# Two arrays of matrix parts move from the constants' end of SBUF to its far end

## The chip, the cores and the metric

The kernel runs on one core of a Trainium2 chip. The metric is device time in microseconds (us) of one execution, with the median over several runs. SBUF, the on-chip memory, has 128 partitions; a tile takes the same byte range in each, so a place in SBUF is a byte offset within a partition.

## The reference

Two layers of an encoder for 256 tokens of width 2048, all in float32. What is computed in each layer, cut to its products:

```python
h = rms_norm(x, norm1_g)
q, k, v, gu, gv = split(h @ w_in)                     # 2048 x 3584
attn = banded_window_attention(rope(norm(q)), rope(norm(k)), v, sink)
sgu  = gelu(gu) * (w_s @ layer_norm(gelu(gv)) + b_s)
x = x + concat(rms_norm(attn), rms_norm(sgu)) @ w_o   # 2048 x 2048
g, u = split(conv3(rms_norm(x, norm2_g) @ w_up))      # 2048 x 11264
x = x + (silu(g) * u) @ w_down                        # 5632 x 2048
```

Nearly all of the work is the products with the weights.

## The kernel before

Every float32 weight is split into a hi part, which the array takes in its faster 4-byte format (fp32r), and a lo part, the rest. A product is then three matmuls: activation-hi by weight-hi, activation-lo by weight-hi, activation-hi by weight-lo.

**The stream of weights.** Weights come from HBM in blocks of 1 MB, 128 partitions by 2048 numbers, on the SyncE (SP) queue, into one of four raw buffers (pool `rawp`). ScalarE (ACT) copies a block into `his`, rounded to fp32r, and VectorE (DVE) subtracts that from the raw block into `los` (`lo_part`, line 154). `his` and `los` are each one tile of six places, taken in turn: `narrow` hands out pieces of 1024 numbers, `wide` of 2048. The copies into `his` are line 169 (`split_narrow`), line 180 (`split_wide`), and lines 262 and 269 (`seven`).

**The products.** TensorE (PE) streams a part as the moving operand, 512 columns at a time, against activations of 128 by 128 numbers that stand still. Lines 208 and 213 do this for the input and output projections (`rows_by_cols`), line 226 for `w_up` and most of `w_down` (`direct`), lines 286, 287 and 292 for the rest of `w_down` (`seven`, a scheme with seven products in place of eight, whose sums of raw blocks, lines 266 to 268, are made by VectorE into a raw buffer). Lines 341 and 346 (`unit`, for `gu`) turn it round: the weight part stands still and the activation is streamed. Activations and everything short-lived lie in 54 slots of 2048 bytes a partition (pool `slots`, tiles called `sl`).

**Order.** A scheduler places instructions by their order in the code and by priorities (`urgent`), and sets the semaphores; the pools set the places in SBUF, one pool behind the other in the order in which they are opened. `const` is opened first, then `lay` (a layer's parameters), `slots`, `rawp`, `small`. The first tile in `const` is `xr`, the residual stream, then `his` and `los`.

Of the kernel before, what the change touches and what calls it, by code (L numbers as in the profile page):

```python
# [9 lines left out]
F32R = mybir.dt.float32r  # L10
# [5 lines left out]
P = 128  # L16
# [11 lines left out]
W = 512  # L28
# [10 lines left out]
PLACES = 6  # L39
# [28 lines left out]
def encoder(ctx: ExitStack, tc: tile.TileContext, xT, x, w_in, w_gu, w_o, w_up, w_down, wsT, pcol, prow, rope, out):  # L68
    nc = tc.nc
    pool = lambda name, bufs, **kw: ctx.enter_context(tc.tile_pool(name=name, bufs=bufs, **kw))  # L70
    const = pool("const", 1)
    lay = pool("lay", 2)
    slots = pool("slots", 54)
    rawp = pool("rawp", 4)
    small = pool("small", 2)
    mmp = pool("mmp", 3, space=bass.MemoryType.PSUM)
    tpp = pool("tpp", 2, space=bass.MemoryType.PSUM)
# [21 lines left out]


    xr = const.tile([P, 2, D], F32, tag="xr", name="xr")
    his = const.tile([P, PLACES * 2 * W], F32R, tag="his", name="his")
    los = const.tile([P, PLACES * 2 * W], F32R, tag="los", name="los")

    def urgent():
        return tc.high_priority(offset=AHEAD)
# [26 lines left out]
    nc.scalar.activation(mhalf, ones[:, :8], AF.Copy, scale=-0.5)  # L133


    turn = {"narrow": 0, "wide": PLACES // 2 - 1}

    def raw_tile():
# [976 lines left out]
```

## Time and profile before

| | |
|---|---|
| median of 3 runs | 2011.28 us (2010.79 to 2011.39) |
| the profiled execution | 2011.29 us |
| its span, first to last instruction | 2009.5 us |
| TensorE matmuls busy | 2003.2 us, 8820 instructions |
| VectorE busy | 1355.6 us |
| ScalarE busy | 1329.3 us |
| transfers: share of 16 engines on the main queue | 64.1% |
| granted TensorE clock | 1.00 |

The profile page gives busy time by engine, the chain of work that ended last, and groups of instructions by line, engine, operation and tile ("los<-raw,his" writes `los` and reads `raw` and `his`). In a group, the numbers after the first bar are busy time in all and the mean ns of one; after the second bar the engine's idle time just before them and what ended it. A matmul's length is the time through the array's pipe, of which several overlap, so the pace is read from the length of a long run of them divided by their number.

### The profile page before, as it was taken

The numbers are of one execution on the slowest core, as the hardware profiler recorded it, in microseconds if no ns is written. First come the engines' busy times: TensorE is split into PE (matmuls) and PEld (weight loads), VectorE is DVE, ScalarE is ACT, GpSimd is POOL, SyncE is SP. The second block draws the span as 40 slices with busy tenths as digits, with TensorE's granted clock in tenths as the row PEclk, the third lists the DMA queues.
The fourth block names the chain that finished last, engine by engine and source line by source line (L and its number), as shares of the span: only waits on it lengthen the run. The fifth ranks groups of instructions, "written<-read, shape, count | busy, mean of one in ns | idle before, by whom it ended". The sixth has DMA issues, their size and how long they took to land.

```text
span 2009.5 us, 23117 instructions
## 1 busy us (share of the span) xinstructions
PE 2003.2 (100%) x8820; PEld 1620.3 (81%) x8820; DVE 1355.6 (67%) x1672; ACT 1329.3 (66%) x1461; POOL 22.4 (1%) x25
## 2 busy tenths in 40 slices
PE   9999999999999999999999999999999999999999
PEld 7888788888888888888888888888888888888887
DVE  5769675666875556678466796655769745666773
ACT  6677487776645777776566864777865457777742
POOL 0100000000000000000000000000000000000000
PEclk9999999999999999999999999999999999999999
DMA  9654676676566776647567446867665667666572
GB/s 354 211 192 147 201 242 197 214 225 194 186 213 212 211 226 208 216 147 264 189 197 245 137 178 193 241 201 224 211 197 189 212 207 231 204 215 209 167 254 82
DMA packets 191311, 414.04 MB, mean 206 GB/s; under 512 B 139488, under 2 KB 140768, under 8 KB 146656
## 3 DMA queue, kind: packets, MB, share of 16 engines
q1 hardware_dynamic: 190480, 411.83, 64.1%
q8 instruction: 69, 1.13, 0.2%
q10 hardware_dynamic: 720, 0.73, 0.1%
q14 instruction: 42, 0.34, 0.1%
HBM read 378.43 MB, written 2.10 MB: 189 GB/s over the span
## 4 chain that ended last, share of the span: by engine, by line
PE 99%; DVE 1%; DMA 0%; issue 0%; SPq 0%; POOL 0%; ACT 0%; DVEq 0%
PE mm L226 66%; PE mm L208 13%; PE mm L213 7%; PE mm L341 3%; PE tp L226 2%; PE mm L346 1%; PE mm L292 1%; PE mm L287 1%; PE mm L286 1%; PE tp L286 0%; PE tp L287 0%; PE tp L292 0%; PE tp L384 0%; PE tp L614 0%; PE tp L385 0%; PE tp L386 0%
## 5 line engine op out<-in xcount | busy, mean ns | idle before, releaser
L154 DVE TENSOR_TENSOR los<-raw,his 128x2048 fp32r<-128x2048 f32 (+3 forms) x468 | 852.9, 1829 | 551.4 <-ACT his L180 399.4
L226 PE MATMUL mm<-his,sl 128*128 128x512 f32 x3808 | 927.8, 396 | 0.0
L226 PEld LDWEIGHTS mm<-his,sl 128*128 128x128 f32 x3808 | 715.3, 188 | 173.2
L180 ACT ACTIVATE his<-raw 128x2048 fp32r<-128x2048 f32 x248 | 466.6, 1882 | 237.6 <-PE mm L226 206.1
L226 PE MATMUL mm<-los,sl 128*128 128x512 f32 x1904 | 483.5, 396 | 0.0
L226 PEld LDWEIGHTS mm<-los,sl 128*128 128x128 f32 x1904 | 357.7, 188 | 86.6
L208 PE MATMUL mm<-his,sl 128*128 128x512 f32 x1152 | 318.2, 397 | 0.2 <-ACT his L169 0.2
L169 ACT ACTIVATE his<-raw 128x1024 fp32r<-128x1024 f32 (+1 forms) x180 | 186.1, 1038 | 168.5 <-PE mm L208 131.8
L208 PEld LDWEIGHTS mm<-his,sl 128*128 128x128 f32 x1152 | 215.8, 188 | 51.8 <-ACT his L169 0.7
L511 ACT COPY sl<-sl 128x1024 uint16<-128x1024 uint16 x98 | 132.8, 1355 | 114.2 <-DMA sl<-sl 114.2
L213 PE MATMUL mm<-los,sl 128*128 128x512 f32 x576 | 181.9, 396 | 1.0 <-DVE los L154 1.0
L213 PEld LDWEIGHTS mm<-los,sl 128*128 128x128 f32 x576 | 108.0, 188 | 27.3 <-DVE los L154 1.5
L914 ACT ACTIVATE sl<-sl,pc 128x256 f32<-128x256 f32 x176 | 95.4, 590 | 0.9
L935 ACT COPY sl<-sl 128x1024 uint16<-128x1024 uint16 x88 | 92.0, 1046 | 2.7
L915 DVE SCALAR_TENSOR_TENSOR sl<-sl,pc 128x255 f32<-128x255 f32 x176 | 77.4, 478 | 4.7 <-ACT sl L914 4.3
L918 DVE SCALAR_TENSOR_TENSOR sl<-sl,pc 128x255 f32<-128x255 f32 x176 | 77.4, 478 | 0.1
L341 PE MATMUL mm<-sl,his 128*128 128x512 f32 x256 | 63.4, 396 | 0.0
L933 ACT ACTIVATE sl<-mm,yr 128x512 f32<-128x512 f32 x88 | 59.8, 679 | 5.3 <-PE mm L226 5.3
L372 ACT ACTIVATE sl<-sl 128x256 fp32r<-128x256 f32 x88 | 31.7, 407 | 46.6 <-DVE sl L963 46.3
L341 PEld LDWEIGHTS mm<-sl,his 128*128 128x128 f32 x256 | 47.0, 188 | 10.3
L269 ACT ACTIVATE his<-raw 128x2048 fp32r<-128x2048 f32 x20 | 38.2, 1912 | 25.7 <-DVE raw L268 23.5
L365 DVE SCALAR_TENSOR_TENSOR sl<-sl,pc 128x256 fp32r<-128x256 f32 x96 | 42.2, 480 | 11.7 <-ACT sl L364 11.6
(145 smaller groups left out, 1172.8 us busy)
## 6 DMA issues: line engine op xcount, KB each, us to landing
raw<-in_w_up SPq DMA_DIRECT2D x176, 1024.0 KB, 5.0
raw<-in_w_down SPq DMA_DIRECT2D x84, 1024.0 KB, 4.6
raw<-in_w_in SPq DMA_DIRECT2D x38, 1024.0 KB, 5.2
raw<-in_w_o SPq DMA_DIRECT2D x32, 1024.0 KB, 4.9
raw<-in_w_gu SPq DMA_DIRECT2D x16, 1024.0 KB, 5.6
raw<-in_w_down SPq DMA_DIRECT2D x8, 512.0 KB, 3.3
sl<-sl SPq DMA_TRANSPOSE x244, 4.2
sl<-in_prow SPq DMA_DIRECT2D x12, 256.0 KB, 7.1
```

The lines of the kernel that those rows point to most:

```text
L154: nc.vector.tensor_tensor(out=lo, in0=part, in1=hi.bitcast(F32), op=ALU.subtract)
L169: nc.scalar.activation(hi[:, cs], part, AF.Copy)
L180: nc.scalar.activation(hi[:, :n], raw[:, :n], AF.Copy)
L208: nc.tensor.matmul(ps[m], acts[kk][:, part, m * P : (m + 1) * P], hi, start=first and kk == 0 and part == 0, stop=False,)
L213: nc.tensor.matmul(ps[m], acts[kk][:, 0, m * P : (m + 1) * P], lo, start=False, stop=last and kk == KB - 1)
L226: nc.tensor.matmul(ps[m], acts[kk][:, part % 2, m * P : (m + 1) * P], w, start=first, stop=done and kk == len(acts) - 1 and part == 2,)
L341: nc.tensor.matmul(ps[:, i, :], part_of(0, k, i), x1, start=k == 0, stop=False)
L511: nc.scalar.copy(words, tall.rearrange("p (b a) n -> p b (a n)", b=2))
L914: nc.scalar.activation(t[:, i, :], s[:, i, :], AF.Identity, bias=col(3), scale=col(1))
L915: nc.vector.scalar_tensor_tensor(out=t[:, i, 1:], in0=s[:, i, : SEQ - 1], scalar=col(0), in1=t[:, i, 1:], op0=ALU.mult, op1=ALU.add)
L918: nc.vector.scalar_tensor_tensor(out=t[:, i, : SEQ - 1], in0=s[:, i, 1:], scalar=col(2), in1=t[:, i, : SEQ - 1], op0=ALU.mult, op1=ALU.add)
L935: nc.scalar.copy(h, rows.bitcast(U16).rearrange("p (j n b) -> p j b n", j=2, b=2))
```

## The change

The two tiles get a pool each, opened behind `rawp`, and are taken from those. Nothing else in the code is touched.

```diff
     slots = pool("slots", 54)
     rawp = pool("rawp", 4)
+    hip = pool("hip", 1)
+    lop = pool("lop", 1)
     small = pool("small", 2)
...
     xr = const.tile([P, 2, D], F32, tag="xr", name="xr")
-    his = const.tile([P, PLACES * 2 * W], F32R, tag="his", name="his")
-    los = const.tile([P, PLACES * 2 * W], F32R, tag="los", name="los")
...
+    his = hip.tile([P, PLACES * 2 * W], F32R, tag="his", name="his")
+    los = lop.tile([P, PLACES * 2 * W], F32R, tag="los", name="los")
     turn = {"narrow": 0, "wide": PLACES // 2 - 1}
```

What stands where then, in bytes of a partition:

| | before | changed |
|---|---|---|
| `xr` | 1,152 to 17,536 | the same |
| `his` | 17,536 to 42,112 | 173,472 to 198,048 |
| `los` | 42,112 to 66,688 | 198,048 to 222,624 |
| other constants | 66,688 to 71,840 | 17,536 to 22,688 |
| layer parameters | 71,840 to 79,264 | 22,688 to 30,112 |
| slots | 79,264 to 189,856 | 30,112 to 140,704 |
| raw buffers | 189,856 to 222,624 | 140,704 to 173,472 |
| small tiles | 222,624 to 224,584 | the same |

On each of the five engines the instructions of the changed kernel stand in the same order as before and wait for the same semaphores; only line numbers behind line 74 differ. Which of the 54 slots a given tile gets may differ too.

## The prediction

> **What bounds the kernel now.** I read the page's busy times first, then the chain that ended last, then its long pieces, then the groups of the instructions that touch the two moved arrays, then who waits for whom.
>
> ```profile
> span 2009.5 us, 23117 instructions
> PE 2003.2 (100%) x8820; PEld 1620.3 (81%) x8820; DVE 1355.6 (67%) x1672; ACT 1329.3 (66%) x1461; POOL 22.4 (1%) x25
> PE 99%; DVE 1%; DMA 0%; issue 0%; SPq 0%; POOL 0%; ACT 0%; DVEq 0%
> ```
>
> TensorE is busy for 2003.2 of 2009.5 us, and 99% of the chain that ended last is its matmuls. A busy TensorE need not be at its best pace, so the pace itself has to be read. The long pieces of the chain give it (start, length, what, how many):
>
> ```profile
> 122.69 7.00 PE mm L341 x30
> 133.43 5.36 PE mm L341 x23
> 163.92 6.31 PE mm L341 x27
> 274.93 235.20 PE mm L226 x1008
> 595.53 291.20 PE mm L226 x1248
> 1141.23 7.46 PE mm L341 x32
> 1972.25 33.62 PE tp L226 x144
> ```
>
> 291.20 us for 1248 matmuls is 233.33 ns each, and 235.20 for 1008 is 233.33 again. Each sends 512 columns of a moving operand. (The 396 ns that the groups give for one is how long it takes through the pipe; a new one starts every 233.33 ns.) TensorE has hardly any gap to win or to lose against another engine; its own waits, named by what ended them, are these:
>
> ```profile
> PE tp L124 <- DVE ones L120: 1.1, 1, 1.1
> PE mm L213 <- DVE los L154: 1.0, 1, 1.0
> PE tp L614 <- DVE sl L606: 0.3, 1, 0.3
> PE mm L208 <- ACT his L169: 0.2, 1, 0.2
> ```
>
> In the whole run TensorE waited 1.2 us for a hi or lo part. So a change of places in SBUF can act on the time in two ways only: it alters the 233.33 ns, or it makes ACT or VectorE so slow that they stop being hidden.
>
> **The change, part by part.** *What it removes, adds and moves.* No instruction is added or removed, and on all five engines the rows stand in the same order with the same waits. `his` and `los` (24,576 bytes a partition each) go from bytes 17,536 to 66,688 up to 173,472 to 222,624. The constants behind them, the layer tiles, the 54 slots and the four raw buffers all come down by 49,152 bytes. So three prices have to be found: TensorE reading `his` and `los` at the top, TensorE reading the slots lower down, and ACT, VectorE and the transfers working on raw, `his` and `los` as neighbours.
>
> *TensorE's reads.* Four groups hold most of them:
>
> ```profile
> L226 PE MATMUL mm<-his,sl 128*128 128x512 f32 x3808 | 927.8, 396 | 0.0
> L226 PE MATMUL mm<-los,sl 128*128 128x512 f32 x1904 | 483.5, 396 | 0.0
> L208 PE MATMUL mm<-his,sl 128*128 128x512 f32 x1152 | 318.2, 397 | 0.2 <-ACT his L169 0.2
> L341 PE MATMUL mm<-sl,his 128*128 128x512 f32 x256 | 63.4, 396 | 0.0
> ```
>
> Lines 226 and 208 stream `his` or `los` and hold a slot tile still. Line 341 does it the other way round: the moving operand is a slot (a region from byte 79,264 to 189,856) and the standing weights are `his`. That is the natural experiment that the profile of before already contains: the streamed operand lies some 60 to 170 thousand bytes higher and starts on a multiple of 32 bytes, no longer of 128. Its pieces give 7.00/30 = 233.3, 7.46/32 = 233.1, 5.36/23 = 233.0 and 6.31/27 = 233.7 ns, where lines of `his` and `los` give 233.33. The pace doesn't know where the streamed operand lies, up to byte 189,856. Two thirds of the new `his` is under that mark; the rest of it and all of `los` go where only raw buffers lay, which TensorE does not stream. For that region I bound the pace by the two ends of the line-341 pieces, 233.0 and 233.7 ns. Over all 8820 matmuls (too many rather than too few, since 8820 counts the slot-streaming and narrow ones too) that is 8820 x (233.33 - 233.0) = 2.9 us less and 8820 x (233.7 - 233.33) = 3.3 us more. I take 0, as the pieces long enough not to be rounded all say 233.33.
>
> *Whether other engines' traffic disturbs the stream.* The new neighbourhood (raw, `his`, `los` in one run of 81,920 bytes at the top) could matter if TensorE's reads shared something with the writers. Three stretches with very different traffic answer it:
>
> ```profile
> 1500.00:1600.00 100.00, 100.00 (x430) 80.49 (x430) 82.19 (x81) 57.08 (x48) 0.00 (x0) 1.00 0.57 197
> 1600.00:1700.00 100.00, 100.00 (x430) 80.51 (x429) 57.67 (x54) 65.26 (x61) 0.00 (x0) 1.00 0.70 215
> 1975.00:2005.00 30.00, 30.00 (x131) 24.13 (x130) 8.34 (x5) 5.74 (x3) 0.00 (x0) 1.00 0.02 8
> ```
>
> The columns are length, then TensorE's matmuls, its weight loads, VectorE, ScalarE and GpSimd, then the granted clock, the transfers' share and GB/s. VectorE at 82%, at 58% and at 28%, transfers at 0.57, 0.70 and 0.02, and TensorE has 430, 430 and 131 matmuls under way in them: 100 us at 233.33 ns are 428.6, 30 us are 128.6, and one or two more are still in the pipe at the left edge. The clock is 1.00 in all three. The last long piece above, 33.62 us for 144 or 233.5 ns with the last one's drain, is mostly that last stretch, with almost nothing else running. Traffic doesn't bend the pace, so its new place shouldn't. Price: 0.
>
> *ACT and VectorE at the new places.* The split of one block is an ACT copy into `his` (line 180) and a VectorE subtraction into `los` (line 154).
>
> ```profile
> L154 DVE TENSOR_TENSOR los<-raw,his 128x2048 fp32r<-128x2048 f32 x260 | 595.5, 2290 | 434.9 <-ACT his L180 399.4 <-ACT his L269 35.4
> L154 DVE TENSOR_TENSOR los<-raw,his 128x1024 fp32r<-128x1024 f32 x180 | 217.2, 1221 | 101.7 <-ACT his L169 79.2 <-PE mm L346 8.4 <-PE mm L226 7.9
> L266 DVE TENSOR_TENSOR raw<-raw x20: 1215/1218/1225, 485.1 to 1911.8; 128x1024 f32<-128x1024 f32 x20
> L180 ACT ACTIVATE his<-raw 128x2048 fp32r<-128x2048 f32 x240 | 458.1, 1909 | 228.1 <-PE mm L226 206.1 <-PE tp L226 11.1 <-PE mm L287 6.6
> L269 ACT ACTIVATE his<-raw x20: 1901/1914/1921, 503.5 to 1918.2; 128x2048 fp32r<-128x2048 f32 x20
> ```
>
> Line 266 reads two operands and writes one, all in raw buffers, that is at the top of memory, where the arrays will be: 1218 ns for 1024 elements. Line 154 reads raw and `his` and writes `los`, far apart: 1221 ns for the same 1024. So having everything in the top region costs nothing; at most 1225/1218, or 0.6%, either way. What covers it: VectorE and ACT are idle for a third of the span, and before its large subtractions VectorE itself waited 434.9 us for ACT. If 0.6% did come on top, it would be 0.006 x 852.9 (all of line 154 on the page) = 5 us of VectorE's time against 650 idle. On the path lies 1% of the chain, about 20 us, and 0.6% of that is 0.1 us. Price: 0 to 0.1 us either way. The order is unchanged, so if this cover were gone nothing else would come late before the blocks themselves.
>
> *The transfers.* Raw moves by 49,152 bytes; sizes, queue and order stay. They wait for the buffer, not the buffer for them:
>
> ```profile
> SPq L178 <- DVE los L154: 811.5, 200, 9.4
> raw<-in_w_up SPq DMA_DIRECT2D x176, 1024.0 KB, 5.0
> ```
>
> The queue stood for 811.5 us in 200 waits until a raw buffer was read out, and a megabyte then lands in 5.0 us. TensorE needs 24 matmuls x 233.33 = 5.6 us for a block, with four buffers in turn. Even a landing that is a few tenths longer is taken up there. Price: 0.
>
> **The sum.** 0 + 0 + 0 + 0. The profiled execution took 2011.29 us, 1.8 of it outside the span of 2009.5; the median of the three runs is 2011.28, so the two are one number. Forecast: 2011.3, with -2.9 and +3.3 at the ends, 2008.4 to 2014.6.
>
> **The rivals.** *Faster: the pace of 233.33 ns contains a conflict that the old place caused.* [...] By rows, the quickest that the profile shows is this short piece:
>
> ```profile
> 149.88 1.39 PE mm L341 x6
> ```
>
> 1.39/6 = 231.7 ns; that for all 8820 gives 14.4 us less, 1997. Against it: line 341 streams from elsewhere in memory and has the same pace, and the same pace holds under heavy and light traffic. A conflict that is the same to a hundredth of a ns for every pair of places would have to be none. [...] Chance 6%. It shows from 4.0 us on, 0.46 ns for each matmul.
>
> *Slower: the splits become the bound.* The mechanism: with raw, `his` and `los` side by side at the top, VectorE's reads and writes there collide with TensorE's stream and with ACT, and line 154 gets longer. It decides first in 1500 to 1600 us, where VectorE is at 82.19 of 100 and these instructions on `his` are
>
> ```profile
> 1500.00:1600.00 100.00, 70.16 (x284) 53.05 (x284) 50.21 (x26) 44.20 (x26) 1.00 0.57 197
> ```
>
> 50.21 us of it: the 17.8 us left are gone when line 154 is longer by 17.8/50.21 = 35%. Were it to take twice as long everywhere, VectorE alone would need 1355.6 + 852.9 = 2208.5 us, and the run 2210. Against it: line 266 works wholly in that region while TensorE streams, and takes what line 154 takes. Also here belongs the small form, that a stream from the top costs TensorE over 0.46 ns more per matmul. Chance 8% together.
>
> *The change does nothing to the chip's work*, because places in SBUF don't matter to it: that is my forecast, 86%.
>
> **How the numbers follow.** About 0.2%, 4.0 us, is what a measurement of this kernel can tell from no change. Same 0.86, faster 0.06, slower 0.08. The range is that of the likeliest case, 2008.4 to 2014.6: it leaves out the two rivals, 14% together.
>
> **What the profile of the changed kernel would show.** Right: the long pieces of line 226 again at 233.33 ns (1248 in 291.20), line 154's 2048 form at 2290 ns within 15, line 180's at 1909 within 15, TensorE's waits for `los` and `his` under 3 us in all, the clock 1.00. Wrong: any other pace in those pieces, which would tell that the streamed operand's place does count above byte 189,856; or VectorE's busy time well over 1356 us and waits of TensorE on line 154 in hundreds of us, which would be the second rival. If pieces of line 226 split into two paces, one for `his` and one for `los`, only part of the top region is different.

## The result: faster by 2.6%, where no change was forecast

The changed kernel takes 1959.12 us (1958.58 to 1959.26) against 2011.34 us for the kernel before in the same session: a ratio of 0.974, 95% interval 0.9728 to 0.9752. That is 52 us less, far outside the stated range of 2008.4 to 2014.6.

The page of the changed kernel, its busy times (the same lines as those shown of before):

```profile
span 1957.4 us, 23117 instructions
PE 1950.2 (100%) x8820; PEld 1619.1 (83%) x8820; DVE 1353.4 (69%) x1672; ACT 1326.1 (68%) x1461; POOL 21.3 (1%) x25
```

VectorE and ScalarE are busy as long as before, within 3.2 us, and so is the weight load (PEld). Only the matmuls lost time: 2003.2 became 1950.2 us with the same 8820 instructions. The long pieces of the chain that ended last (start, length, what, how many; all line numbers are two higher now) say where:

```profile
119.97 6.82 PE mm L343 x30
130.62 5.24 PE mm L343 x23
269.87 228.48 PE mm L228 x1008
581.31 282.88 PE mm L228 x1248
1921.09 32.65 PE tp L228 x144
```

282.88/1248 = 226.67 ns from one matmul to the next, where it was 233.33: 6.67 ns less, in every long run alike. Line 343, which streams a slot and holds `his`, went the same way, from 233.3 to 6.82/30 = 227.3. The gain was not bought from another engine. The instructions that write the arrays and TensorE's waits for them, and two stretches that answer to the two busy ones of before:

```profile
L156 DVE TENSOR_TENSOR los<-raw,his 128x2048 fp32r<-128x2048 f32 x260 | 594.8, 2290 | 398.1 <-ACT his L182 362.5 <-ACT his L271 35.2
L182 ACT ACTIVATE his<-raw 128x2048 fp32r<-128x2048 f32 x240 | 458.3, 1911 | 174.1 <-PE mm L228 150.8 <-PE tp L228 10.6 <-DVE xr L319 7.0
```

```profile
PE mm L215 <- DVE los L156: 1.2, 1, 1.2
PE tp L124 <- DVE ones L120: 1.1, 1, 1.1
```

```profile
1460.00:1560.00 100.00, 100.00 (x443) 82.84 (x442) 83.77 (x82) 59.32 (x50) 0.00 (x0) 1.00 0.58 202
1560.00:1660.00 100.00, 100.00 (x443) 82.84 (x442) 59.32 (x54) 65.66 (x61) 0.00 (x0) 1.00 0.71 219
```

A subtraction into `los` takes 2290 ns as before, a copy into `his` 1911 (1909). Under 84% and 59% of VectorE there are 443 matmuls in 100 us each time, 13 more than before, at the same granted clock of 1.00.

**Does the pace carry the whole gain?** 8004 matmuls stream `his` or `los` over 512 columns and 256 of line 343 hold `his`: 8260 x 6.67 ns = 55.1 us. The spans differ by 2009.5 - 1957.4 = 52.1 us. Of the missing 3 us, the starts of the matmuls in the trace place 1.9 in the projections of lines 210 and 215, which wait a little more (397.7 us in all, from 407.3, where the pace alone would give 395.8), 0.9 in line 343, and 0.6 in the narrow matmuls of line 348, which got slower; against these 3.4, line 124 at the start takes 0.6 less. The matmuls of line 348 are the only ones that stream 256 columns; their group before and after:

```profile
L346 PE MATMUL mm<-sl,los 128*128 128x256 f32 x256 | 33.8, 282 | 0.0
```

```profile
L348 PE MATMUL mm<-sl,los 128*128 128x256 f32 x256 | 34.4, 285 | 0.0
```

### The profile page after: what moved, and what is told of

It is laid out like the page before. It is cut to its first block, busy times and chain, and to the rows that moved or that the text cites. A ratio compares the mean times of both kernels' runs of the same rounds, so it can differ in the third digit from the quotient of the medians.

```text
span 1957.4 us, 23117 instructions
## 1 busy us (share of the span) xinstructions
PE 1950.2 (100%) x8820; PEld 1619.1 (83%) x8820; DVE 1353.4 (69%) x1672; ACT 1326.1 (68%) x1461; POOL 21.3 (1%) x25
## 4 chain that ended last, share of the span: by engine, by line
PE 97%; DMA 1%; DVE 1%; issue 0%; SPq 0%; ACT 0%; POOL 0%; DVEq 0%; ACTq 0%
PE mm L228 66%; PE mm L210 12%; PE mm L215 6%; PE mm L343 3%; PE tp L228 2%; PE mm L348 2%; PE mm L288 1%; PE mm L294 1%; PE mm L289 1%; DMA raw<-in_w_in 1%; DMA qk<-in_prow 1%; PE tp L289 0%; PE tp L294 0%; PE tp L288 0%; PE tp L386 0%; PE tp L616 0%
## 5 line engine op out<-in xcount | busy, mean ns | idle before, releaser
L228 PE MATMUL mm<-his,sl 128*128 128x512 f32 x3808 | 902.4, 389 | 0.0
L228 PE MATMUL mm<-los,sl 128*128 128x512 f32 x1904 | 470.8, 389 | 0.0
L210 PE MATMUL mm<-his,sl 128*128 128x512 f32 x1152 | 311.0, 391 | 0.6 <-ACT his L171 0.5
L215 PE MATMUL mm<-los,sl 128*128 128x512 f32 x576 | 178.3, 390 | 1.2 <-DVE los L156 1.2
```

The source lines that it names most:

```text
L210: nc.tensor.matmul(ps[m], acts[kk][:, part, m * P : (m + 1) * P], hi, start=first and kk == 0 and part == 0, stop=False,)
L215: nc.tensor.matmul(ps[m], acts[kk][:, 0, m * P : (m + 1) * P], lo, start=False, stop=last and kk == KB - 1)
L228: nc.tensor.matmul(ps[m], acts[kk][:, part % 2, m * P : (m + 1) * P], w, start=first, stop=done and kk == len(acts) - 1 and part == 2,)
```

## The experiments

### Is it the region, or the distance between the two operands of a matmul?

Of the places in SBUF, two things changed together: the region of the arrays, and the distance between an array and the slots that stand against it. Each slot is 2048 bytes and each array a multiple of that, so the distance of their starts is the same for all pairs, modulo 2048, up to the steps of 512 bytes with which a slot's blocks of 128 numbers begin. Before, the start of `his` less that of the slots was 17,536 - 79,264, which is 288 short of a multiple of 2048, or 224 past a multiple of 256; for line 341, which streams a slot and holds `his`, it is the other way round, 288 past and 32. In the changed kernel both are multiples of 2048. Theory A: the distance decides. Theory B: the region does. Theory C: the arrays' own alignment does. Theory D: the traffic of the other engines.

**Low end, distance mended** (kernel before, two unused tiles):

```diff
+    const.tile([P, 72], F32, tag="pad1", name="pad1")
     his = const.tile([P, PLACES * 2 * W], F32R, tag="his", name="his")
     los = const.tile([P, PLACES * 2 * W], F32R, tag="los", name="los")
+    const.tile([P, 440], F32, tag="pad2", name="pad2")
```

> The kernel before, with 288 unused bytes ahead of the two arrays and 1760 behind them: the arrays stay at the low end (from byte 17,824), the slots start at 81,312, and the distance of arrays and slots is a multiple of 2048 bytes as in the changed kernel. Theory A: the changed kernel's time, 1959 us within 3, line of the long runs at 226.67 ns. Theory B: 2011 us, 233.33 ns. Theory C: 1959 too, since the arrays' starts are now 32 behind a multiple of 128.

Measured: 1959.37 us, ratio 0.9741 (0.9725 to 0.9757).

**Far end, distance of before** (changed kernel, an unused tile in a pool between `rawp` and `hip`):

```diff
     rawp = pool("rawp", 4)
+    padp = pool("padp", 1)
     hip = pool("hip", 1)
...
+    padp.tile([P, 440], F32, tag="pad1", name="pad1")
     his = hip.tile([P, PLACES * 2 * W], F32R, tag="his", name="his")
```

> The changed kernel with 1760 unused bytes between the raw buffers and the two arrays: these stay at the far end, but their distance from the slots is again 288 bytes off a multiple of 2048, as before the change. Theory A: 2011 us within 3 and 233.33 ns. Theory B: 1959 us and 226.67 ns. Theory C: 2011, since the arrays start at a multiple of 128 again.

Measured: 2010.90 us, ratio 1.000 (0.999 to 1.0009). One long piece of the chain of each, the mended low end first:

```profile
583.23 282.88 PE mm L228 x1248
```

```profile
595.05 291.20 PE mm L230 x1248
```

226.67 and 233.33 ns. The region has no part in it (B falls): the arrays run fast where they always lay and slowly at the far end. The traffic's new neighbourhood has none either (D falls), since at the far end raw, `his` and `los` are neighbours in both.

**The least cure.** The same as the low end, with 32 bytes ahead of the arrays and 224 behind (`[P, 8]` and `[P, 56]`):

> The kernel before with 32 unused bytes ahead of the two arrays and 224 behind them, and nothing else changed: everything stays in its old region, and arrays and slots differ by a multiple of 256 bytes, though not of 2048. If 256 bytes is the period in the whole kernel too, 1959 us within 3 and long runs at 226.67 ns; if the period is longer there, between 1959 and 2011.

Measured: 1959.85 us, ratio 0.9743 (0.9727 to 0.976), and

```profile
580.82 282.88 PE mm L228 x1248
```

256 unused bytes a partition, with everything in its old region, bring all of it. So the period is not longer than 256 bytes in the whole kernel.

### The spacing against the distance

**First sweep.** A kernel that only copies part of the input, and has TensorE do bursts of matmuls out of one large tile:

```python
for i in range(24):
    at = s + 128 * (i % 4)
    nc.tensor.matmul(t[:, i // 2 % 2, :n], big[:, at : at + 128], big[:, m : m + n], ...)
```

> Computes nothing of the reference: 182 bursts of 24 fp32r matmuls with a new weight load for each, all operands in one large tile, and only the start addresses of the streamed and of the standing operand differ from burst to burst (streamed start minus standing start in steps of 32 and of 4 bytes; both moved together by 32 to 96 bytes; 16 pairs of regions, each at a distance that is a multiple of 2048 bytes and at one that is 288 bytes off such a multiple; and 256 columns in place of 512). No other engine works on the tile while they run. Theory A (what counts is the distance of the two operands' starts, modulo some power of two: 288 bytes off a multiple of 2048 before, 0 in the changed kernel): spacing changes with the distance, about 226.7 ns at 0 and 233.3 ns at 288 bytes, in every pair of regions and however both are moved together. Theory B (the region counts): spacing differs between pairs of regions, with 233.3 ns where the streamed start is under 66,688 bytes and 226.7 where it is above 173,472, at any distance. Theory C (the streamed operand's own alignment to 128 bytes counts: 0 before, 32 in the changed kernel): spacing changes when both are moved together. Theory D (traffic of ACT and VectorE into the arrays sets it): one spacing for all.

(There were 154 bursts, not 182.) Its page shows that TensorE was almost alone once the tile was filled: VectorE copies 8 columns of each burst's result, 167 ns, and nothing else runs.

```profile
PE 845.6 (96%) x3696; PEld 687.0 (78%) x3696; DVE 25.7 (3%) x154; ACT 45.5 (5%) x26; POOL 0.2 (0%) x4
```

The mean ns from start to start over a burst's last 20 matmuls, by the distance of streamed from standing start modulo 256 bytes, 512 columns:

```
distance   0      32     64     96     128    160    192    224
ns         227.2  233.35 228.75 233.95 233.35 234.35 233.35 233.35
```

These eight values come back in each of the eight blocks of 256 bytes that were swept, to 0.1 ns; only the very first burst, whose first matmuls start every 427 ns, is left out. At 0 most bursts begin with three to eight slower gaps (230, 236, 228, 233, 231) and then run at 226.67, so their means lie between 226.65 and 227.8. Moving both operands by 32, 64 or 96 bytes gave 227.7, 233.3, 228.75, 233.95 for 0, 32, 64, 96 each time, so C falls, and all 16 pairs of regions gave 227.7 to 227.8 at 0 and 233.30 to 233.35 at 288, the distance of line 341; that of the arrays before, 224 modulo 256, is in the table, with the same 233.35. In steps of 4 bytes the value goes up and down with no plain rule: 226.65 at 28 and 60, 236.65 at 4, 240.0 at 20.

With 256 columns the order turns round: 119.65 ns at 0 and 117.75 at 32, which is what lines 346 and 348 did.

**Does the table foretell whole kernels?** Two distances put into the changed kernel by a pad of `[P, 16]` and `[P, 40]` at the place shown above, the second chosen because it should be worse than before:

> The changed kernel with 64 unused bytes ahead of the two arrays, so that their distance from the slots is 64 bytes off a multiple of 256. If the distance modulo 256 bytes of the two operands sets the spacing, as the first sweep has it (228.75 ns at 64, 233.3 at 192 = -64 for line 341, where the roles are changed, 226.67 at 0), the 8004 matmuls that stream the arrays cost 2.08 ns more each, 16.7 us, and the 256 of line 341 1.7 us: 1977.5 us within 5. If only multiples of 32 that are not multiples of 64 were bad (alignment to 64 bytes): 1959. If any offset is as bad as the 288 bytes of before: 2011.

> The same with 160 unused bytes. By the sweep's spacing at that distance (234.35 ns against 226.67; 233.95 for line 341 at -160 = 96): 8004 x 7.68 ns = 61.5 us and 1.9 us more than the changed kernel, 2022.5 us within 5, and so slower than the kernel before by 0.6%. If any offset is as bad as that of before: 2011.

Measured at 160: 2018.85 us, ratio 1.0037 (1.0024 to 1.005): slower than before, as expected, and 3.7 us under the number. At 64 the times fell in two groups, 1977.0 and 1977.2, 1991.4 and 1991.8 us, the first at the number. A long piece of the 64-byte kernel's profiled execution, which took 1977.01 us, and one of the 160-byte kernel:

```profile
586.46 285.65 PE mm L230 x1248
```

```profile
597.40 292.38 PE mm L230 x1248
```

228.89 and 234.28 ns, where the sweep had 228.75 and 234.35.

**The second group.** The 64-byte kernel was profiled twice more.

> The 64-byte kernel once more, for one profile. Its earlier times fell in two groups, 1977.1 and 1991.6 us; the profiled one was of the first, with 228.9 ns in the long runs. If this one falls in the second group, the trace shows whether the long runs of line 226 have another spacing (14.5 us over 8004 matmuls would be 1.8 ns, 230.7 ns) or TensorE waits somewhere.

> The same as the run before it, for a second chance of the other group: 228.9 ns and 1977 us, or 230.7 ns (or waits) and 1991.6 us.

The first took 1976.58 us, the second 1991.27, so the second group has a trace. Pieces of its chain:

```profile
271.12 230.72 PE mm L230 x1008
585.61 285.65 PE mm L230 x1248
1253.64 235.20 PE mm L230 x1008
1574.24 291.20 PE mm L230 x1248
```

The first layer's long runs have 228.89 ns and the second's 233.33, not one value of 230.7 as I had reckoned; TensorE's longest wait in it is 1.2 us, as in the other. So at 64 bytes the chip knows two steady rhythms. The two traces part at 1189 us, in the second layer's output projection, where two short matmuls of line 416 break the stream. Just ahead of that both have gaps of 226, 229 and 232 ns. Behind the break the first execution has one of 314 ns and then 229, 232, 226 again; the second has 322 and then 232, 233, 233, 234. That stays through the 3414 matmuls to the end, which take 781.3 and 796.5 us: 15.2 us, and the group's whole difference, as the second was 0.5 us ahead there. So the rhythm was set where the stream started again after a break; the profiled execution of 1977.01 us had 320 ns there and fell into the quick one, so the length of that gap alone doesn't tell which. What decides was not found; the six repeats of distances 0 and 64 in the third sweep below showed one rhythm each.

### What clashes with what

**Second sweep**: the standing operand read at other steps, with fewer columns, and bf16.

> Computes nothing of the reference: 111 bursts of 32 matmuls that ask what the clash is between. Standing operands read at a step of 1, 2, 4 or 8 numbers; of 128, 96, 64 or 32 columns; one standing block in place of four in turn; bf16 operands; 128, 256 and 384 streamed columns; and distances of 132 to 252 bytes in steps of 4. Theory A1 (the streamed operand's reads clash with the weight load's reads, which run beside them): the spacing changes with the step of the standing operand, and shrinks towards 512 columns at 2.4 per ns, 213.3 ns, as the weight load gets shorter, at every distance: half the excess at 64 columns, a quarter at 32. Theory A2 (the excess of 226.67 ns over 213.3 at the best distance is the streamed operand's own, and only the rest a clash): 226.67 ns stays for 32 columns. For bf16 both expect less excess, since half the bytes are read. One block or four: no difference.

(108 bursts.) With 128 standing columns at a step of 1 number the first table came back, but for 128 bytes, where two of three bursts ended at 232.4 ns and not at 233.3: a second distance with more than one rhythm. At a step of 2 the spacing over the last 24 matmuls was 230.0 to 235.0 ns, with 0 bytes now among the slow ones (233.3) and 160 among the best; at 4, 233.3 to 240.0; at 8, 243.3 to 247.0. So the addresses from which weights are loaded do seem to take part. The step of 2 speaks most clearly for it, as the load itself then takes 193 to 197 ns where it took 188; at 4 and 8 it takes 309 and 330, and that alone could slow the rest. One standing block in place of four changed nothing. With 32 columns, whose load takes 108 ns, the spacing of the last 16 was 226.6 to 231.6: the excess does not shrink with the length of the weight load, against what I expected of A1, and 226.67 stays the floor, as A2 has it. The 2.4 columns per ns in the text agree with what the runs gave: in the first sweep 256 and 512 columns at distance 0 were 119.65 and 226.67 ns, 107.0 for 256 columns more, and the widths of the third sweep below give 53.3 for 128. From 4-byte steps between 132 and 252 came 226.67 ns again at 156, 236, 240 and, once settled, 252, never less, and 240.0 at 196 and 244. For bf16 all eight distances gave 215.8 ns; the two groups on the page of groups:

```profile
L63 PE MATMUL mm<-narrow 128*128 128x512 bf16 x256 | 55.4, 379 | 0.0
L63 PE MATMUL mm<-big 128*32 128x512 f32 x128 | 29.7, 392 | 0.0
```

55.4/256 = 216 ns for bf16 and 29.7/128 = 232 ns for 32 fp32r columns, mean of four distances.

**Third sweep**: whose weights matter, and whether their addresses do.

> Computes nothing of the reference: 42 bursts of 96 fp32r matmuls. In the first eight the standing operand's start alternates every 8 matmuls between two distances from the streamed one. If the streamed operand clashes with the weight load that runs beside it (that of the next matmul), the spacing changes one or more matmuls ahead of the change of distance; if it clashes with its own, at it. Ten bursts load 128 times the same column in place of 128 columns: if the weight load's addresses take part, the spacing no longer follows the distance as before; if the distance acts only through the streamed start, it does. Widths of 320 to 508 columns at 0 and 32 bytes: a fixed cost for each matmul gives 53.3 ns per 128 columns and an intercept of 13.3 ns at distance 0; a rate below 2.4 columns per ns gives a steeper line. The last six bursts repeat distances 0 and 64: whether one distance has more than one steady spacing, as the two groups of times of the 64-byte kernel (1977 and 1991.6 us) suggest.

Loading one column 128 times gave 231.05 ns at all ten distances, to 0.01: without addresses that run along, the distance has no effect. And with the standing start changed every eight matmuls between distances 0 and 32, the gaps to the next start were, ns by place in the period of 16 (places 0 to 7 at distance 0, 8 to 15 at 32):

```
0 to 7    227  226  227  227  226  227  227  235
8 to 15   233  234  231  235  233  234  231  227
```

The gap of place 7, whose own weights are at the good distance, is already slow (235 ns); that of 15 is already fast (227). The distance that counts is the one to the weights of the next matmul, which are loaded while this one streams: in the changed kernel's trace the next load starts 3 ns after a matmul's start, by the median, and in line 228 takes 188 of the 226.67 ns. So the clash is between two things TensorE does at once, the stream and the next weight load beside it; where in the chip they meet, no run shows. For bf16 the distance made no difference (215.8 ns at all eight), for fp32r it did: 226.6 to 240.0 ns, by nothing but the distance. A bf16 load is shorter (98 ns for 188), but the 32-column fp32r loads, 108 ns, are nearly as short and still leave 226.6 to 231.6. For widths of 256, 320, 352, 384 and 512 columns at distance 0 the spacing was 119.7 to 120.0, 146.67, 160.00, 173.33 and 226.67: 53.3 ns for each 128 columns, or 2.4 columns per ns, and 13.3 on top. Between 416 and 508 it lies up to 3.4 ns above that line. That fp32r is the faster 4-byte format for the array can be read from the kernel before: each of the 32 products of plain float32 in line 830, 128 columns wide, stands in the trace as two matmuls 112 ns apart by the median, so about 224 ns, while the 256 fp32r columns of line 346 take 118.

### One array at a time

```diff
     xr = const.tile([P, 2, D], F32, tag="xr", name="xr")
+    los = const.tile([P, PLACES * 2 * W], F32R, tag="los", name="los")
...
     his = hip.tile([P, PLACES * 2 * W], F32R, tag="his", name="his")
-    los = lop.tile([P, PLACES * 2 * W], F32R, tag="los", name="los")
```

That is `his` moved alone; the other kernel is its mirror image, with `los` moved alone.

> Half of the change: `his` goes behind the raw buffers, `los` stays among the constants. The distance of `his` from the slots is then 0 modulo 256 bytes, that of `los` 32 off. If each matmul's spacing follows from the distance of its own streamed array, only the 2668 matmuls that stream `los` stay at 233.33 ns: 2668 x 6.67 = 17.8 us above the changed kernel, less 0.6 us for the 256 narrow ones of the `gu` projection, 1976.3 us within 4, with two spacings in the trace, 226.67 where `his` is streamed and 233.33 where `los` is. If it is a matter of the arrays as neighbours, or of all operands being congruent, there is one spacing.

> The other half: `los` goes behind the raw buffers, `his` stays. By the same theory the 5336 matmuls that stream `his` and the 256 of `gu` that hold it stay at 233.33 ns: 5592 x 6.67 = 37.3 us above the changed kernel, 1996.4 us within 4. The two halves would add up to about the whole change, 52 us.

Measured: 1985.10 us (ratio 0.9868, 0.9852 to 0.9885) and 2002.97 us (0.9957, 0.9943 to 0.9972). The direction is right and both are more than expected, by 8.8 and 6.6 us. Alone they gain 26.3 and 8.4 us, together 34.7, less than the 52 of the whole. The shortfall is in the switches between the arrays. TensorE's rows in a stretch of the kernel with only `his` moved:

```profile
1401.23 3.81 PE L227 MATMUL mm<-his,sl 128*128 128x512 f32 x16
1404.88 2.03 PE L227 MATMUL mm<-los,sl 128*128 128x512 f32 x8
1406.75 3.81 PE L227 MATMUL mm<-his,sl 128*128 128x512 f32 x16
```

From the start of 16 hi matmuls to that of the 8 lo ones are 3.65 us, 228.1 ns each, and back 1.87, 233.8. The gaps one by one after a switch to `his`, means of the 239 switches of this line to a stretch of 16, are 230.0, 235.8, 228.3, 232.5, 230.8, and only then 226.6, 226.6, 226.8, the same settling as in the bursts of the sweep. Five gaps sum to 1157.4 ns, 24 more than 5 x 226.67. 239 switches x 24 ns = 5.7 us, and the hi matmuls of that line do sum to 890.9 us from start to start here and 884.9 in the changed kernel, 6.0 more. Of the other 2.8 us, over what the two spacings would give, 1.5 lie in the projections (lines 209 and 214), 0.6 in the lo matmuls of line 227 and 0.6 in lines 287 and 288. With only `los` moved, the five gaps after each switch to `los` are the same within 0.1 ns, and the lo matmuls of line 227 sum to 448.1 us for 442.2: 5.9 of the 6.6. A switch doesn't always cost this much. In line 209, with stretches of four, the gaps after it are 234.2, 227.3, 227.3 and 227.2, and in the alternating bursts above the first gap at the good distance was already 227. In those bursts the streamed start stayed the same and only the standing one moved; whether that is why wasn't tested.

## Why the prediction was wrong

- **"The pace doesn't know where the streamed operand lies"** is the step that failed. The sentence is true of the place and was used for the distance. Line 341 was taken for a natural experiment because its operand is streamed from another region; but it has the same two regions with the roles changed, so its distance is that of the other lines with the sign changed: 32 bytes modulo 256, where theirs is 224. The sweep gives 233.35 ns at 32 and at 224. The two kinds of matmul agreed because two bad distances happen to cost the same, not because nothing is at stake. With a good distance the same lines run at 226.67 ns, and 8260 matmuls times 6.67 ns are the 52 us that the sum put at 0 (55, of which waits and the narrow matmuls took back 3).
- **The bounds of 233.0 and 233.7 ns** were taken from the spread of short pieces of that one kind, so they bounded rounding and not the cost. A value outside, 226.67, was in no row of before since no long run there had a good distance.
- **"A conflict that is the same to a hundredth of a ns for every pair of places would have to be none"** failed with it. Tile sizes that are multiples of 2048 give every pair the same distance; a conflict set by distance is then just that constant.
- **The faster rival** had the right kind of mechanism, with 6%. Its size was off: 1997 us by the quickest piece, 231.7 ns, where 226.67 ns and 1959.12 us came. The bf16 matmuls of the second sweep started every 215.8 ns; of the 17.5 ns by which the fp32r matmuls of before were slower than those, distance accounts for 6.67 and the other 10.9 stayed at the best distance that was tried.
- **Traffic, splits, transfers and order** were priced right: 0. The 2048 form of line 154 stayed at 2290 ns, line 180 at 1911, waits for `his` and `los` at under 3 us. The sign by which the text wanted to tell the case apart, another pace in the long pieces, is what came, though it was put down there to the region above byte 189,856, which has no part in it.
- **The slower rival's** splits never came near. Its small form, more ns per matmul from a change of places, exists: at 160 bytes the kernel is slower than before.

## What to carry to other kernels

When TensorE is the bound with fp32r operands streamed 512 columns at a time, look at the start-to-start spacing of its matmuls, and compare the start addresses of streamed and standing tiles modulo 256 bytes: a pad of 32 and 224 bytes was worth 2.6% here. Try a distance of 0 first (226.67 ns here, where 32 and 224 bytes gave 233.35), for all arrays that alternate, since each switch to a good distance from a bad one cost some 24 ns in the long runs with one array moved; and let tiles be multiples of 256 bytes so that one pad sets all pairs. A perfectly even pace isn't proof that nothing is in the way: before a group in the trace is used as a natural experiment, check that the suspected quantity, here a difference of two addresses, really differs in it.

## What the runs showed of the hardware that I had not expected

- fp32r matmuls of 512 columns start every 226.6 to 240.0 ns, by the distance of the streamed start from that of the next weights modulo 256 bytes; bf16 ones every 215.8 ns at each of eight distances.
- For 512 fp32r columns a floor was reached at 226.67 ns, 13.3 ns above 512 columns at the 2.4 per ns that the widths gave, and neither a distance nor a shorter weight load went below it. What it consists of stays open, and so does the rule by which the distance acts: the values at 4-byte steps were measured, not explained.
- The rhythm has a memory: at 64 bytes 228.89 and 233.33 ns are both steady, for 3414 matmuls behind one break in the stream. Two executions of one program differ by 14.7 us for it, at a granted clock of 1.00.
- Traffic of VectorE, ScalarE and the transfers did not move the spacing by 0.1 ns: 226.67 and 233.33 ns in the kernels, with the arrays at either end and VectorE busy for 58 to 84 of 100 us, and 226.67 and 233.35 in the bursts with almost nothing else running.
